# Mixer products with tokens stationary and 512 weight columns moving, and the second-last expert's combining moved into the last expert's up product

## Chip, cores and metric

One core of a Trainium2 chip runs the whole kernel in one launch. The metric is device microseconds of one execution, the median over runs. The kernel before took 1434.71 us (three runs, 1433.88 to 1435.99).

## Reference

256 tokens of width 1024 pass through one layer. A combined projection of the stream feeds three mixers (gated DeltaNet, a gated recurrent block "LRU", sliding-window attention "SWA"). Each mixer's result is projected to width 1024, multiplied by a sigmoid gate, and the sum goes through one output projection; then a layer norm, 32 experts with top-4 routing, and a last sublayer. Cut to what matters here:

```python
proj = h @ w_in
(qa, ka, va, za, aa, ba, xl, gl, qc, kc, vc, gate_logits) = split_cols(proj, IN_SPLITS)
y_a = gdn_branch(qa, ka, va, za, ...) @ w_o_gdn      # ends: o * rms(o) * norm_w * silu(z)
y_b = lru_branch(xl, gl, ...) @ w_o_lru
y_c = swa_branch(qc, kc, vc, ...) @ w_o_swa
g_a, g_b, g_c = jnp.split(jax.nn.sigmoid(gate_logits), 3, axis=-1)
y = (g_a * y_a + g_b * y_b + g_c * y_c) @ w_out
x = layer_norm(DEEPNORM_ALPHA * x + y, ...)
# then per token: sum over its 4 experts of gate * (clamped_swiglu(x @ w_gu[e] + b_gu[e]) @ w_down[e] + b_down[e])
```

## The kernel before

**Numbers as two halves.** Each fp32 operand of a mixer product is split into a rounded part (HI, xh, ...) and the rest (LO, xl, ...), both of type fp32r; a product is three matmuls: hi by hi, hi by the tokens' rest, the weights' rest by hi.

**Units.** `column` (L341) makes one unit of PE work: 128 columns of a 1024-row weight matrix are the stationary operand, k block by k block, and all 256 tokens move, so 8 x 3 = 24 matmuls of 256 columns go into one PSUM tile `pjt` (two buffers, pool `pj`). The result has weight columns on partitions and tokens along the free side. There are 117 units in a fixed order (L1195 to L1230): the input columns of the mixers, gate 1, `w_o_lru`, VA, gate 2, `w_o_swa`, six of gate 0, eight z columns, two of gate 0, eight of `w_o_gdn`, and eight of the output projection. The last (`out_unit`, L1086) already holds 128 tokens stationary and moves 256 columns of `w_out`.

**What a unit needs and leaves.** SyncE loads each unit's 512 KB piece three ahead (`load`, L361) into four buffers `w`; `split` (L369) makes HI on ACT and LO on DVE (640 columns) and POOL (384), into a ring of three. After a unit its evacuation runs: `evac_gate` (a tanh on ACT into `TG`), `evac_merge` (two DVE operations that gate and add into `MG`; for the last branch also the split into MH and ML), `evac_z` (gating by silu(z), split into AH and AL), or the residual and norm statistics of `out_unit`.

**What sets the order.** `run` (L384) writes the program out unit by unit: first the evacuation of the unit before, then the split of the piece for two units later, then the 24 matmuls, then one step of each "strand" (attention, the DeltaNet chunks, norms, router), which puts small PE work between units. Where a unit is marked `drain` (first of `w_o_gdn`, first output unit), all pending evacuations are written out ahead of it. Each engine executes its own list in that order:

```python
for u in range(-2, len(units) + 1):
    steps(pend)                       # evacuation of unit u-1, first part
    ... load(done + 3); split(...)    # piece for unit u+2
    products(ps)                      # 24 matmuls
    steps(strands)                    # small work between units
```

**Turns.** `normed` (L876) ends the DeltaNet heads: it norms rows in token layout and turns them by four transposes of 128x128 to the column layout, four times.

**Experts.** After the router, `moe` streams 32 experts' weights, 12.6 MB each, through ten buffers of 2 MB: four of them (`F`) are filled during the mixer (`prefetch`), six (`w5` to `w0`) lie on mixer memory and are loaded when that is free. Per expert `expert` (L1406) does the up product (64 matmuls of 512 columns), the activation, the down product (32 matmuls); `spread` (L1473) brings the result back to its tokens by six matmuls per half of the tokens and adds it into Y. The spread of expert e-1 is done inside expert e: the first half between the up product and the first turn, the second between the two halves of the down product (`fill`, L1582).

Of the kernel before, what the change touches and what calls it, by code (L numbers as in the profile page):

```python
# [111 lines left out]
def mixer(mx, tc, nc, a, xs, rt, dram, cst, ones, el):  # L112
# [6 lines left out]
    pj = mx.enter_context(tc.tile_pool(name="pj", bufs=2, space=PSUM))  # L119
# [34 lines left out]
    banks = Slots([bank(i) for i in range(6)])  # L154
# [14 lines left out]
    lns = mpa.tile([P, 2, 4, 6], F32, name="lns")  # L169
# [171 lines left out]
    def column(src, c0, bh, bl, evac, needs=(), drain=False):  # L341

        hl, i = [], (len(units) + 2) % 3

        def dst():
            hl.extend((HI[:, i], LO[:, i]))
            return hl

        def products(ps):
            b = [f() for f in (bh, bl)]  # L350
            for k in range(KD):
                for n, (l, r) in enumerate(((0, 0), (0, 1), (1, 0))):
                    pe.matmul(ps, hl[l][:, k], b[r][:, k], start=k == 0 and n == 0, stop=k == KD - 1 and n == 2)  # L353

        order.append((len(pieces), len(units) - 2))
        pieces.append((src[:, :, c0:c0 + P], dst))
        units.append((products, evac, needs, drain))
# [3 lines left out]
    def load(n):  # L361
        if n < len(order):
            i = order[n][0]
            raw[i] = wp.tile([P, KD, P], F32, name="w", tag="w")
            sync.dma_start(raw[i], pieces[i][0])
# [3 lines left out]
    def split(i):  # L369
# [3 lines left out]
        n = share[0]  # L373
        if n:
            dve.tensor_sub(lo[:, 0:n], s[:, 0:n], hi[:, 0:n].bitcast(F32))  # L375
        if n < KD:
            pool.tensor_tensor(out=lo[:, n:], in0=s[:, n:], in1=hi[:, n:].bitcast(F32), op=ALU.subtract)  # L377
# [6 lines left out]
    def run():  # L384
        pend, done = [], 1
        for u in range(-2, len(units) + 1):
            cur[0] = u
            if u < len(units) and u >= 0 and units[u][3]:
                steps(strands)
                for g in pend:  # L390
                    for _ in g:
                        pass
                pend = []
# [6 lines left out]
            if 0 <= u < len(units):  # L400
                products, evac, needs, _ = units[u]
                assert all(n in events for n in needs), (u, needs)
                ps = pj.tile([P, T], F32, name="pjt", tag="pj")
                products(ps)
                pend = [evac(ps)]
# [80 lines left out]
    def evac_gate(b):  # L486
        def f(ps):
            if b == 0:
                M["TG"] = big("TG", [P, KD, T])
            act.activation(M["TG"][:, b], ps, AF.Tanh, scale=0.5)  # L490
# [3 lines left out]
    def evac_merge(b, first=False, last=False):  # L494
        def f(ps):
            if b == 0 and first:
                M["MG"] = big("MG", [P, KD, T])
            if b == 0 and last:
                M["MH"] = big("AT", [P, KD, T], F32R)
                M["ML"] = big("U", [P, KD, T], F32R)  # L500
            tg, dst = M["TG"][:, b], M["MG"][:, b]
            if first:
                dve.scalar_tensor_tensor(dst, tg, 1.0, ps, ALU.add, ALU.mult)
                return
            dve.scalar_tensor_tensor(tg, tg, 1.0, ps, ALU.add, ALU.mult)
            dve.tensor_add(dst, dst, tg)
            if last:
                yield
                act.copy(M["MH"][:, b], dst)
                dve.tensor_sub(M["ML"][:, b], dst, M["MH"][:, b].bitcast(F32))  # L510
            yield
# [364 lines left out]
    def normed(t, h4, o, on=None):  # L876
# [9 lines left out]
        if on is None:  # L886
            on = yield from rows_.take()
# [3 lines left out]
        yield  # L891
        ps = yield from banks.take()
        for i in range(4):
            pe.transpose(ps[:, i * P:(i + 1) * P], on[:, i], ident)
        yield
        rows_.done(on)
        act.copy(KQ[:, c0, 0, t * P:(t + 1) * P], ps.rearrange("p (h c) -> p h c", h=4))
        banks.done(ps)
# [124 lines left out]
    def evac_z(b):  # L1023
        def f(ps):
# [726 lines left out]
```

## Time and profile before

| | |
|---|---|
| median of 3 runs | 1434.71 us |
| profiled execution | 1434.07 us |
| its span, first to last instruction | 1432.3 us |
| PE busy | 1348.4 us (94%), 8472 matmuls |
| DVE, ACT, POOL busy | 607.2, 374.6, 248.7 us |
| mean granted TensorE clock | 0.987 |
| moved | 481.77 MB, mean 336 GB/s |

Stages, by the units' start: mixer products from 9.8 to 456 us, norm and router to 469 us, experts to 1389 us, the last sublayer to the end. Busy time of PE is modelled: matmuls overlap, so the distance from start to start tells what one costs, and the mean time of one is longer than that.

### The profile page before, as it was taken

Reading aid. Unit: us, or ns where it says so; the run is one execution under the profiler, and the core shown is the slowest. Engines: PE = TensorE matmul, PEld = TensorE weight load, DVE = VectorE, ACT = ScalarE, POOL = GpSimd, SP = SyncE. Lnnn points to the kernel's source line nnn. Section 1 sums busy time; section 2 is a strip of 40 time slices with the busy share of each in tenths; the row PEclk is TensorE's granted clock in tenths of the full one; section 3 lists DMA queues with packets and bytes.
Section 4 is the critical chain, followed back from the end, with each engine's and each line's share of the span. In section 5 each row is a group of like instructions: output and inputs, shape, how many; then the busy total and the mean of one; then the engine's idle time right before and its main releaser. Section 6 shows DMA issues by size and latency. Waiting matters only on the chain. (4 is left out here: it accounts for less than half of the span.)

```text
span 1432.3 us, 20918 instructions
## 1 busy us (share of the span) xinstructions
PE 1348.4 (94%) x8472; PEld 788.8 (55%) x8473; DVE 607.2 (42%) x1289; ACT 374.6 (26%) x771; POOL 248.7 (17%) x217
## 2 busy tenths in 40 slices
PE   8989989999999899999999999999999999889987
PEld 7989988899988433433433333333333433333335
DVE  6497984865585222322322222223222322222238
ACT  6766464644551110110110111011100110011121
POOL 5654864434561000000000000000000000000000
PEclk9999999999999899999999999999999999999999
DMA  8745565445898799999999999999999999999970
GB/s 257 220 134 136 128 183 159 119 132 178 262 293 327 305 416 428 427 429 427 430 426 428 428 429 428 427 430 428 428 427 427 430 429 427 428 426 430 429 330 30
DMA packets 171292, 481.77 MB, mean 336 GB/s; under 512 B 11340, under 2 KB 134876, under 8 KB 137784
## 3 DMA queue, kind: packets, MB, share of 16 engines
q1 hardware_dynamic: 169592, 477.16, 84.6%
q0 software_dynamic: 848, 1.86, 0.4%
q8 instruction: 68, 1.11, 0.3%
q10 hardware_dynamic: 752, 1.38, 0.3%
q14 instruction: 32, 0.26, 0.0%
HBM read 478.78 MB, written 3.42 MB: 337 GB/s over the span
## 5 line engine op out<-in xcount | busy, mean ns | idle before, releaser
L1419 PE MATMUL gu<-w,xe 128*64 128x512 f32 x1168 | 262.9, 598 | 6.9 <-DMA w<-in_w_gu_dram 6.9
L353 PE MATMUL pjt<-xh,HI 128*128 128x256 f32 x680 | 199.8, 294 | 12.7 <-DVE cv L419 6.1
L1419 PE MATMUL gu<-F,xe 128*64 128x512 f32 x880 | 199.1, 596 | 5.0 <-DMA F<-in_w_gu_dram 5.0
L377 POOL TENSOR_TENSOR LO<-w,HI 128x384 fp32r<-128x384 f32 (+1 forms) x111 | 166.4, 1501 | 174.9 <-ACT HI L372 172.0
L353 PE MATMUL pjt<-xh,LO 128*128 128x256 f32 x680 | 193.6, 285 | 2.6 <-DVE LO L375 2.5
L353 PE MATMUL pjt<-xl,HI 128*128 128x256 f32 x680 | 193.4, 284 | 0.0
L1419 PEld LDWEIGHTS gu<-w,xe 128*64 128x64 f32 x1168 | 81.8, 137 | 165.6 <-issue 144.4
L1437 DVE TENSOR_SCALAR gc<-gu 128x256 f32<-128x256 f32 x64 | 27.0, 422 | 273.2 <-PE gu L1419 273.2
L353 PEld LDWEIGHTS pjt<-xh,HI 128*128 128x128 f32 x680 | 131.3, 193 | 18.3 <-issue 4.7
L375 DVE TENSOR_TENSOR LO<-w,HI 128x640 fp32r<-128x640 f32 (+1 forms) x111 | 112.8, 1017 | 62.2 <-ACT HI L372 60.7
L1350 POOL DMA_DIRECT2D pt<-in_p_dram x1 | 0.8, 779 | 789.7 <-DVE lc L1441 789.7
L353 PEld LDWEIGHTS pjt<-xh,LO 128*128 128x128 f32 x680 | 131.3, 193 | 3.1 <-DVE LO L375 2.7
L353 PEld LDWEIGHTS pjt<-xl,HI 128*128 128x128 f32 x680 | 131.5, 193 | 0.3
L1454 PE MATMUL dn<-w,hT 128*64 128x512 f32 x560 | 128.5, 601 | 1.5 <-ACT hT L1447 1.5
L1490 DVE TENSOR_TENSOR Y<-Y,cb 128x512 f32<-128x512 f32 x124 | 79.5, 683 | 114.2 <-PE cb L1479 114.2
L372 ACT CAST HI<-w 128x1024 fp32r<-128x1024 f32 x111 | 115.5, 1041 | 43.2 <-PE pjt L353 17.7
L1419 PEld LDWEIGHTS gu<-F,xe 128*64 128x64 f32 x880 | 60.4, 137 | 119.6 <-issue 105.6
L1454 PE MATMUL dn<-F,hT 128*64 128x512 f32 x464 | 106.0, 598 | 0.0
L1438 ACT ACTIVATE sg<-gc 128x256 f32<-128x256 f32 x64 | 26.8, 419 | 285.0 <-DVE gc L1437 285.0
L1382 PE MATMUL gat<-oh,xs 128*128 128x128 f32 x512 | 76.3, 294 | 24.8 <-DVE oh L1390 20.0
L1382 PEld LDWEIGHTS gat<-oh,xs 128*128 128x128 f32 x512 | 64.4, 197 | 44.5 <-issue 27.8
L1427 DVE TENSOR_TENSOR gt<-gwt,gt 128x256 fp32r<-128x256 f32 x32 | 13.6, 425 | 152.2 <-ACT gt L1426 152.2
(404 smaller groups left out, 1622.0 us busy)
## 6 DMA issues: line engine op xcount, KB each, us to landing
w<-in_w_gu_dram SPq DMA_DIRECT2D x73, 2048.0 KB, 29.2
F<-in_w_gu_dram SPq DMA_DIRECT2D x51, 2048.0 KB, 29.5
w<-in_w_down_dram SPq DMA_DIRECT2D x70, 1024.0 KB, 19.1
F<-in_w_down_dram SPq DMA_DIRECT2D x58, 1024.0 KB, 20.8
w<-in_w_in_dram SPq DMA_DIRECT2D x85, 512.0 KB, 3.7
F<-in_w_gu_dram SPq DMA_DIRECT2D x8, 1024.0 KB, 6.0
w<-in_w_o_lru_dram SPq DMA_DIRECT2D x8, 512.0 KB, 4.5
w<-in_w_o_swa_dram SPq DMA_DIRECT2D x8, 512.0 KB, 3.8
```

What stands on the lines that cost most here:

```text
L353: pe.matmul(ps, hl[l][:, k], b[r][:, k], start=k == 0 and n == 0, stop=k == KD - 1 and n == 2)
L372: act.copy(hi, s)
L375: dve.tensor_sub(lo[:, 0:n], s[:, 0:n], hi[:, 0:n].bitcast(F32))
L377: pool.tensor_tensor(out=lo[:, n:], in0=s[:, n:], in1=hi[:, n:].bitcast(F32), op=ALU.subtract)
L1350: pool.dma_start(pt, a["p"][0, 0].rearrange("(t p) c -> p t c", p=P))
L1382: pe.matmul(ps[:, kk], xs[:, t, k * P:(k + 1) * P], oh[:, t], start=t == 0, stop=t == 1)
L1419: pe.matmul(gu[64 * j:64 * j + 64, b], xe[:, k], w[:, j * D + b * 512:j * D + (b + 1) * 512], start=False, stop=k == KD - 1)
L1427: dve.tensor_sub(gt[:, 1], ps, gt[:, 0].bitcast(F32))
L1437: dve.tensor_scalar(gc[:, c], guv[:, c, 0], 7.0, None, op0=ALU.min)
L1438: act.activation(sg[:, c], gc[:, c], AF.Sigmoid, scale=1.702)
L1454: pe.matmul(dn[64 * jj:64 * jj + 64], hT[:, 2 * hf + kk, j * 64:j * 64 + 64], w[:, kk, jj * 512:(jj + 1) * 512], start=hf == j == kk == 0, ...
L1490: dve.tensor_add(y, y, pss[jj])
```

## The change

Gates, the three merge products, z and the output projection (64 of 117 units) get a new shape: 128 tokens are the stationary operand and 512 weight columns move. A piece is 256 rows by 512 columns (`wide` makes four units of 12 matmuls for 512 output columns and both token halves, with one evacuation after the fourth). PSUM is divided anew: `pj` has three tiles of 512 (two of 256 before), the strands five banks (six). Results now have tokens on partitions, so the DeltaNet rows stay as they are (`normed` loses its transposes), and `evac_z` and the last `evac_merge` turn their results with four times four transposes each. The output units mix token halves, column halves and k blocks so that the first use only the k blocks of the first half of the merge; the two drains are gone. In the last expert the spread of the expert before moves from `fill` into the up product, after k = 3 and k = 5.

```diff
-    pj = mx.enter_context(tc.tile_pool(name="pj", bufs=2, space=PSUM))
+    pj = mx.enter_context(tc.tile_pool(name="pj", bufs=3, space=PSUM))
...
-    banks = Slots([bank(i) for i in range(6)])
+    banks = Slots([bank(i) for i in range(5)])
...
+    def rows_by(ps, t, kp, b, hl, first=0, last=3):
+        for kk in range(2):
+            for n, (l, r) in enumerate(((0, 0), (0, 1), (1, 0))):
+                pe.matmul(ps, b[r][:, 2 * kp + kk, t * P:(t + 1) * P], hl[l][:, kk * 512:(kk + 1) * 512],
+                          start=kp == first and kk == n == 0, stop=kp == last and kk == 1 and n == 2)
...
+            def products():
+                b = [f() for f in (bh, bl)]
+                if kp == 0:
+                    pss.extend((psum(), psum()))
+                for t in range(2):
+                    rows_by(pss[t], t, kp, b, hl)
+                return pss
+
+            piece(src[:, 2 * kp:2 * kp + 2, c0:c0 + 512], n_ - 2, dst)
+            units.append((products, evac if kp == 3 else idle, needs[kp]))
...
-            if u < len(units) and u >= 0 and units[u][3]:
-                steps(strands)
-                for g in pend:
-                    for _ in g:
-                        pass
-                pend = []
...
+    def evac_gate(c):
+        def f(pss):
...
+            for t in range(2):
+                act.activation(M["TG"][:, t, halves[c]], pss[t], AF.Tanh, scale=0.5)
...
+            for t in range(2):
+                tg, dst = M["TG"][:, t, halves[c]], M["MG"][:, t, halves[c]]
+                if first:
+                    dve.scalar_tensor_tensor(dst, tg, 1.0, pss[t], ALU.add, ALU.mult)
+                else:
+                    dve.scalar_tensor_tensor(tg, tg, 1.0, pss[t], ALU.add, ALU.mult)
+                    dve.tensor_add(dst, dst, tg)
+            yield
+            for t in range(2 if last else 0):
+                b = yield from banks.take()
+                for i in range(4):
+                    pe.transpose(b[:, i * P:(i + 1) * P], M["MG"][:, t, (4 * c + i) * P:(4 * c + i + 1) * P], ident)
+                ps, q = b.rearrange("p (k t) -> p k t", k=4), slice(t * P, (t + 1) * P)
+                hi = M["MH"][:, 4 * c:4 * c + 4, q]
+                act.copy(hi, ps)
+                dve.tensor_sub(M["ML"][:, 4 * c:4 * c + 4, q], ps, hi.bitcast(F32))
...
-        dve.tensor_tensor(out=on, in0=ov, in1=bc(oss[:, t, c0]), op=ALU.mult)
+        dve.tensor_tensor(out=KQ[:, c0, 0, t * P:(t + 1) * P], in0=ov, in1=bc(oss[:, t, c0]), op=ALU.mult)
...
-        for i in range(4):
-            pe.transpose(ps[:, i * P:(i + 1) * P], on[:, i], ident)
...
+                act.activation(th, z, AF.Tanh, scale=0.5)
+                dve.scalar_tensor_tensor(th, th, 1.0, z, ALU.add, ALU.mult)
+                dve.tensor_tensor(out=th, in0=th, in1=o, op=ALU.mult)
+            yield
+            for t in range(2):
+                b = yield from banks.take()
+                for i in range(4):
+                    pe.transpose(b[:, i * P:(i + 1) * P], rows[t][1][:, i], ident)
...
+    for c, kp, u in ((1, 0, -6), (1, 1, -4), (0, 0, -2), (0, 1, -1), (0, 2, 0), (0, 3, 1), (1, 2, 2), (1, 3, 3)):
+        piece(wout[:, 2 * kp:2 * kp + 2, halves[c]], S + u, held_piece(kp) if c else ring_piece(kp))
...
+    for work, done in ((both(0), ()), (both(1), ()), (second(0, 0, 1), ()), (both(2), ()), (both(3), ((0, 0), (1, 0))),
+                       (second(0, 2, 3), ((0, 1),)), (second(1, 0, 1), ()), (second(1, 2, 3), ((1, 1),))):
+        units.append(out_unit(work, done))
...
+            if e == NE - 1 and k in (3, 5):
+                spread(*prev, k // 5)()
...
-                if prev is not None:
+                if prev is not None and e < NE - 1:
                     pending.append(spread(*prev, 0))
...
-            elif prev is not None:
+            elif prev is not None and e < NE - 1:
                 spread(*prev, 1)()
```

How the lists of two engines change. First DVE at the end of `w_o_gdn` and the start of the output units; L375 (after: L426) is a split, L505 and L506 (L552 and L553) gate and add into MG, L510 (L562) makes ML in the tile U. Before, every unit of 24 matmuls has one such set:

```order
L375 TENSOR_TENSOR LO<-w,HI 128x640
L375 TENSOR_TENSOR xl<-w,xh 128x5x128
L510 TENSOR_TENSOR U<-MG,AT 128x256
L505 SCALAR_TENSOR_TENSOR TG<-TG,pjt 128x256
L506 TENSOR_TENSOR MG<-MG,TG 128x256
L375 TENSOR_TENSOR LO<-w,HI 128x640
L510 TENSOR_TENSOR U<-MG,AT 128x256
```

Now one set of four 512-wide operations stands after four units, and ML follows from a turned PSUM tile (`pg`):

```order
L552 SCALAR_TENSOR_TENSOR TG<-TG,pjt 128x512
L553 TENSOR_TENSOR MG<-MG,TG 128x512
L552 SCALAR_TENSOR_TENSOR TG<-TG,pjt 128x512
L553 TENSOR_TENSOR MG<-MG,TG 128x512
L426 TENSOR_TENSOR LO<-w,HI 128x640
L426 TENSOR_TENSOR xl<-w,xh 128x640
L426 TENSOR_TENSOR LO<-w,HI 128x640
L562 TENSOR_TENSOR U<-pg,AT 128x4x128
L426 TENSOR_TENSOR LO<-w,HI 128x640
L562 TENSOR_TENSOR U<-pg,AT 128x4x128
```

The pieces of `w_out` (xl here) no longer come two to a unit, and a merge no longer stands in front of every split. Second, PE in the last expert (gu: up product, gwt and tr: turns, cb<-ob,gt: spread, dn: down product), before and now:

```order
L1419 MATMUL gu<-F_9849,xe 64x512 x4
L1419 MATMUL gu<-F_9864,xe 64x512 x8
L1419 MATMUL gu<-w_9874,xe 64x512 x8
L1479 MATMUL cb<-ob,gt 128x512 x6
L1446 MATMUL tr<-cst,lc 128x128 x2
L1454 MATMUL dn<-w_9884,hT 64x512 x8
L1446 MATMUL tr<-cst,lc 128x128 x2
L1479 MATMUL cb<-ob,gt 128x512 x6
L1454 MATMUL dn<-w_9887,hT 64x512 x8
```

```order
L1485 MATMUL gu<-F_8988,xe 64x512 x4
L1545 MATMUL cb<-ob,gt 128x512 x6
L1485 MATMUL gu<-F_9013,xe 64x512 x8
L1545 MATMUL cb<-ob,gt 128x512 x6
L1485 MATMUL gu<-w_9033,xe 64x512 x8
L1512 MATMUL tr<-cst,lc 128x128 x2
L1520 MATMUL dn<-w_9043,hT 64x512 x8
L1512 MATMUL tr<-cst,lc 128x128 x2
L1520 MATMUL dn<-w_9046,hT 64x512 x8
```

Both spreads now stand between the up product's weight rows, and none between activation and down product.

## Rows read from the trace of the kernel before

**Rows 1.** Busy time by stage (columns as its second line names them), three stretches.

```profile
core 0: us, PE busy (x) PEld busy (x) DVE busy (x) ACT busy (x) POOL busy (x), PEclk, DMA share, GB/s
460.00:480.00 20.00, 18.38 (x88) 13.53 (x90) 6.44 (x36) 3.38 (x9) 0.56 (x1) 0.67 0.59 242
...
600.00:800.00 200.00, 193.71 (x980) 77.69 (x978) 56.56 (x130) 23.82 (x61) 0.00 (x0) 1.00 1.01 428
...
1200.00:1380.00 180.00, 165.40 (x790) 60.67 (x792) 43.91 (x100) 19.96 (x49) 0.78 (x1) 1.00 1.01 427
```

**Rows 2.** Timeline of the DMA queue of SyncE, last mixer loads to first reuse.

```profile
449.49 7.31 SPq L1309 DMA_DIRECT2D w<-in_w_gu_dram  x4
477.88 6.00 SPq L1321 DMA_DIRECT2D F<-in_w_down_dram  x4
```

**Rows 3.** Timeline of PE, gate 0 units: start, busy us, line, operation, count.

```profile
364.68 0.28 PE L353 MATMUL pjt<-xh,HI 128*128 128x256 f32 x1
...
367.56 0.28 PE L353 MATMUL pjt<-xh,HI 128*128 128x256 f32 x1
...
370.44 0.60 PE L894 MATMUL pg<-cst,F 128*128 128x128 f32 x4
370.79 0.36 PE L353 MATMUL pjt<-xh,HI 128*128 128x256 f32 x1
...
373.75 0.28 PE L353 MATMUL pjt<-xh,HI 128*128 128x256 f32 x1
```

**Rows 4.** Timeline of PE in the last sublayer: fp32r matmuls of 512 and 256 columns.

```profile
1399.22 7.74 PE L1654 MATMUL gu<-F,w 128*128 128x512 f32 x32 [0.24 <-ACT w L1644]
...
1412.15 4.82 PE L1654 MATMUL cb<-F,w 128*128 128x512 f32 x20
...
1417.74 2.56 PE L1654 MATMUL cb<-F,w 128*128 128x256 f32 x20
```

**Rows 5.** Timeline of PE: starts of the seventh z unit and second output unit.

```profile
391.03 0.34 PE L353 MATMUL pjt<-xh,HI 128*128 128x256 f32 x1
...
434.85 0.28 PE L1091 MATMUL pjt<-HI,AT 128*128 128x256 f32 x1
```

**Rows 6.** Waits of PE, 388 to 436 us: total, times, longest.

```profile
PE pjt L1091 <- ACT AT L509: 1.2, 1, 1.2
PE pjt L353 <- DVE TG L505: 1.1, 2, 0.7
PE pjt L353 <- DVE th L1032: 0.9, 3, 0.3
```

**Rows 7.** Timeline of DVE and ACT: operations 512 wide, and one slow 256-wide.

```profile
388.76 1.24 DVE L1036 TENSOR_TENSOR KT<-th,RV 128x256 fp32r<-128x256 f32 x1
...
1390.14 0.69 DVE L1490 TENSOR_TENSOR Y<-Y,cb 128x512 f32<-128x512 f32 x1 [0.59 <-PE cb L1479]
...
1397.99 0.59 ACT L1366 COPY w<-cb 128x512 f32<-128x512 f32 x1 [3.47 <-PE cb L1365]
```

**Rows 8.** Waits of PE, 178 to 300 us.

```profile
PE pjt L353 <- DVE LO L375: 2.5, 1, 2.5
...
PE pjt L353 <- ACT TG L490: 1.6, 2, 1.2
```

**Rows 9.** Timeline of DVE after the last output product.

```profile
456.07 0.42 DVE L1095 SCALAR_TENSOR_TENSOR xs<-xs,pjt 128x256 f32<-128x256 f32 x1 [2.78 <-PE pjt L1091]
456.53 0.43 DVE L1096 BATCH_NORM_STATS2 lns<-xs 128x6 f32<-128x256 f32 x1
```

**Rows 10.** Timeline of PE in the last expert.

```profile
1372.99 3.65 PE L1419 MATMUL gu<-w,xe 128*64 128x512 f32 x16 [0.43 <-DMA w<-in_w_gu_dram]
1376.57 0.97 PE L1479 MATMUL cb<-ob,gt 64*128 64x512 f32 x6
...
1378.58 0.48 PE L1446 MATMUL tr<-cst,lc 128*128 128x128 f32 x2 [1.04 <-DVE lc L1441]
...
1383.59 0.96 PE L1479 MATMUL cb<-ob,gt 64*128 64x512 f32 x6
...
1384.48 3.65 PE L1454 MATMUL dn<-w,hT 128*64 128x512 f32 x16
```

More of the change, by code (lines that the diff above doesn't have):

```diff
@@ L339, in mixer, with ring, piece, psum @@
     units, pieces = [], []
-    def column(src, c0, bh, bl, evac, needs=(), drain=False):
-        hl, i = [], (len(units) + 2) % 3
+    def ring(i):
+        i = (i + 2) % 3
+        return [v[:, i].rearrange("p k c -> p (k c)") for v in (HI, LO)]
+    def piece(src, at, dst):
+        order.append((len(pieces), at))
+        pieces.append((src, dst))
+    def psum():
+        return pj.tile([P, 512], F32, name="pjt", tag="pj")
+    def column(src, c0, bh, bl, evac, needs=()):
+        n_ = len(units)
+        hl = []
@@ new lines, in idle, with wide, unit, dst @@
+    def idle(ps):
+        return
+        yield
+    def wide(src, c0, bh, bl, evac, needs=((), (), (), ())):
+        pss = []
+        def unit(kp, n_):
+            hl = []
+            def dst():
+                hl.extend(ring(n_))
+                return hl
+            def products():
+                b = [f() for f in (bh, bl)]
[6 more added lines that the diff above has]
+            units.append((products, evac if kp == 3 else idle, needs[kp]))
+        for kp in range(4):
+            unit(kp, len(units))
@@ L1084, in norm_rows @@
         M["xT"] = big("MG", [P, KD, T])
[L1086 to L1107 removed]
+    out_ps = {}
@@ new lines, in out_unit, with products, evac @@
+    def out_unit(work, done):
+        def products():
+            b = (M["MH"], M["ML"])
+            for t, c, kp in work:
+                if (t, c) not in out_ps:
+                    out_ps[t, c] = psum()
+                hl = [v[:, (kp % 2) * 1024:(kp % 2 + 1) * 1024] for v in M["wo", kp // 2]] if c else M["ring", kp]
+                assert f"m{t}{kp // 2}" in events
+                rows_by(out_ps[t, c], t, kp, b, hl)
+        def evac(_):
+            for t, c in done:
+                xv = xs[:, t, halves[c]]
+                dve.scalar_tensor_tensor(xv, xv, 2.0 * ALPHA, out_ps[t, c], ALU.mult, ALU.add)
+                dve.bn_stats(lns[:, t, c], xv)
+                if c == 0 and t == 0:
+                    for i in range(2):
+                        M["rps", i] = yield from banks.take()
+                    M["wk"] = wp.tile([P, KD * P], F32, name="wk", tag="w")
+                    pool.memset(M["wk"][:, 0:80], -3.0e38)
+                if c:
+                    dve.bn_aggr(mv[:, t, 0:2], lns[:, t])
+                    dve.tensor_scalar(mv[:, t, 2:3], mv[:, t, 1:2], 4 * LN_EPS, None, op0=ALU.add)
+                    pool.tensor_tensor(out=mv[:, t, 2:3], in0=mv[:, t, 2:3], in1=mhalf[:, 0:1], op=ALU.pow)
+                    spawn(first_norm(t))
@@ L1210, in mixer @@
     gate_units(1)
-    for b in R8:
-        column(wo["w_o_lru"], b * P, *B, note("wol" if b == 7 else "", evac_merge(b, first=True)), needs=("lru",))
+    for c in range(2):
+        wide(wo["w_o_lru"], c * 512, *B, note("wol" if c else "", evac_merge(c, first=True)), needs=(("lru",),) * 4)
     for b in R8:
```

173 lines of the change are left out of this document (67 added, 106 removed).

## The prediction

> **What bounds the kernel.** I read the stages first [rows 1]. In the expert stage the DMA engines are full: share 1.01 at 428 GB/s between 600 and 800 us, the same at 427 until 1380, while PE has gaps. Nothing that the change does alters those bytes, so the experts keep their length, and what can move is the time at which their stream starts and what follows its end. The DMA queue shows the start [rows 2]: after four loads at 449.49 us nothing is issued until 477.88, when the first early buffer has been used by expert 0. In that gap the DMA engines run at a share of 0.59 [rows 1]: the buffers are full and the stream waits for PE. So the stream starts when expert 0 does, and expert 0 waits for the mixer's last product, the norm and the router. Whatever PE saves in the mixer moves everything behind it, one for one.
>
> In the mixer PE is the pace where the change works. A gate unit starts at 364.68 and the next at 367.56 us [rows 3]: 2.88 us for 24 matmuls, 0.120 us each, without a gap. The clock there is at its 2.4 GHz level, at which 256 columns take 0.1067 us, so 0.0133 us of each is not columns.
>
> **The sum, step by step.** It is made against the profiled execution, 1434.07 us, which is 0.64 below the median 1434.71.
>
> *Matmul shape.* 64 units of 24 are 1536 matmuls of 256 columns; now 768 of 512, with the same columns in all. Before: 1536 x 0.120 = 184.3 us. The nearest row for the new shape is the last sublayer, also fp32r, 128x128 stationary and 512 moving [rows 4]: 20 of them in 4.82 us, the last lasting 0.395, so (4.82 - 0.395)/19 = 0.233 each. In the same rows 20 of 256 columns take 2.56 us, (2.56 - 0.28)/19 = 0.120, which is the mixer's own number, so the row is comparable. 768 x 0.233 = 178.9 us: **-5.4 us**. Bounds: none if 512 cost twice 256 (0.240); -10.2 us if the 0.0133 us belongs to each instruction and is paid half as often (0.2267 each).
>
> The Trainium skill, "TensorE: Matmul & The Clock Gate", section "Back-to-back issue gap", gives N/2.4 + 2.5 ns, hence 109.2 ns for 256 columns and 215.8 for 512; by it the change saves 2.6 ns a pair, 2.0 us in all, and the sum would come out 3.4 us higher. The trace does not agree with its 256-column figure: 120 ns here.
>
> *Transposes.* z's sixteen take the place of the sixteen in `normed`: nothing. The last merge adds sixteen, in four groups. A group of four costs its unit 370.79 - 367.56 - 2.88 = 0.35 us and delays the next unit, 373.75 - 370.79 - 2.88 = 0.08 [rows 3]: 4 x 0.43 = **+1.7 us**.
>
> *Stalls around z, `w_o_gdn` and the first output unit.* From 391.03 to 434.85 us [rows 5] there are 13 units, 43.82 us where 13 x 2.88 = 37.44 would do: 6.4 us lost. The waits that end last are on DVE for z and the merges and on ACT for the split of the last merged block [rows 6]. All three come from evacuating after every unit, and from the drain. With 512-wide evacuation once in four units, output pieces spread over ten units, and output units that begin on the half already merged, I let all of it go. What is late next is the PSUM tile: a wide unit takes two of three tiles, so the second tile of the next must be free after its first six matmuls, 6 x 0.233 = 1.4 us. The evacuation that frees it is one 512-wide operation, 0.59 us on ACT or 0.69 on DVE, for z both [rows 7]; that is inside 1.4 us, but DVE also has slow executions (1.24 us for 256 columns, [rows 7]). For the 14 wide products I put back 0.15 us each, 2.0 us. Net **-4.4 us**; bounds -6.4 (none put back) and 0.
>
> *Gate 1 and `w_o_lru`.* Between 178 and 300 us PE waits 1.6 us for the tanh of a gate on ACT and 2.5 us for a split on DVE [rows 8]. With two evacuations instead of eight I let half of the first go: **-0.8 us**. The second is DVE's own pace; if DVE sets the stretch, these 16 units cannot give their share of the shape, 16/64 of 5.4, which is the bound on the other side, +1.3 us.
>
> *PSUM banks, pieces and queues.* Five banks for the strands instead of six cost nothing in the order: every DeltaNet and attention step stands after the same or the next unit, and its cover is the unit's matmuls; without that cover a step would wait a full unit, 2.8 us. The pieces have the same 512 KB and the same split. SyncE's loads keep their order; one of the six mixer buffers is free earlier (KQ is no longer used for `w_out`), another later, since RV and KT now serve the very last output unit. The latter delays part of the four loads of 449.49 us by about 4 us, and the 21 us until 477.88 cover that [rows 2].
>
> *End of the mixer.* The last evacuation is 512 wide: one DVE operation and one statistic, 0.42 and 0.43 us before [rows 9], about 0.69 each now [rows 7]: **+0.5 us**, on the path to the router. Bound +1.5: the first token half is also finished two units before the end instead of three.
>
> *Last expert.* Before, the first spread lay under the wait for the activation: up product over at 1376.6, first turn at 1378.58 us. The second stood in the path, 1384.48 - 1383.59 = 0.89 us [rows 10]. Now both lie in the up product, whose last weights PE had waited for 0.43 us: +2 x 0.89 - 0.43 - 0.89 = **+0.5 us**. Bounds: -0.9 if the weights come so late that both are hidden, +0.9 if they come in time.
>
> Sum: -5.4 + 1.7 - 4.4 - 0.8 + 0.5 + 0.5 = -7.9 us. 1434.07 - 7.9 = **1426.2 us**.
>
> **Rivals.**
>
> *The shape gives little.* The longer run of 512-column matmuls in the same rows [rows 4] gives (7.74 - 0.40)/31 = 0.237: then the shape saves 768 x 0.003 = 2.5 us instead of 5.4, and the time is 1429.1 us. For it: that run is the longer one. Against: its first gap holds a start, and the shorter run has none. By the skill's gap above it would be 1429.6 us.
>
> *The clock takes it back.* After the last product PE has little to do until expert 0, and the granted clock falls to its 1.2 GHz level: 0.67 on average between 460 and 480 us, so half speed during 20 x 0.33/0.5 = 13 us [rows 1]. The first half's turns and router products now also lie behind the last product. If a second spell of 13 us falls on expert 0's up product, which is PE work without a wait, it costs half of it, 6.6 us: 1432.8 us, no change. For it: the spell already ends where that product begins. Against: the work of PE behind the last product becomes more, not less.
>
> *A PSUM wait takes the place of the stalls (slower).* If at each of the 14 wide products the tile came free one slow DVE operation too late, 1.24 us [rows 7], PE would wait 17.4 us where I put back 2.0: 1426.2 + 15.4 = 1441.6 us. It decides from 0.9 us per wide product on: 14 x 0.9 = 12.6, less 2.0, eats the 7.9 and 2.9 more. For it: evacuations queue on DVE and ACT behind strand work, and PE has already waited 2.5 us for DVE [rows 8]. Against: outside 178 to 212 us the longest such wait is 0.7 us [rows 6], and DVE's share of the evacuations gets smaller.
>
> **How the numbers follow.** A measurement of this kernel can tell about 0.2% from no change, 2.9 us: below 1431.8 is faster, above 1437.6 slower, counted from the median. The forecast has 0.62 (0.60 faster, 0.02 same); the smaller shape gain 0.15 (0.12 faster, 0.03 same); the clock 0.13 (0.02, 0.10, and 0.01 slower); the PSUM wait 0.10 (0.02 same, 0.08 slower). Together 0.74 faster, 0.17 same, 0.09 slower. For the range, all good ends together give -10.2 + 1.7 - 6.4 - 0.8 + 0.5 - 0.9 = -16.1; I take 1419.5, where about two thirds of the favourable part of the sum's spread is in. Above it reaches past the clock's 1432.8 to 1434.5, and leaves the PSUM wait out.
>
> **What would show it.** Right: in the gate 0 and `w_o_gdn` stretch, starts of 512-column matmuls 0.233 us apart; no PE wait over 0.3 us between the first z unit and the last output unit; the gap in SyncE's queue before the first reuse of an early buffer still there and its end near 470 us instead of 477.88; the expert stage as long as before, at 428 GB/s; the last expert's down product without a spread between its halves, with its up product longer by about 1.3 us. Wrong: starts 0.240 apart; PE waiting for ACT TG or DVE MG at the first unit of each wide product; the half-clock spell reaching into expert 0; or a stream of experts that starts earlier and ends no earlier.

## The result, and the profile after

The changed kernel takes **1420.68 us** (median of 4 runs, 1420.20 to 1421.88); the kernel before, beside it, 1435.35 (1433.88 to 1437.46). The ratio is 0.9894, 95% interval 0.9879 to 0.9909: about 1.1% or 14.7 us faster. The forecast was 1426.2, within 1419.5 to 1434.5. A second series of the unaltered changed kernel gave 1421.51 (six runs, ratio 0.991, 0.989 to 0.993). The profiled execution has a span of 1418.8 us, 13.5 less than before, and this is the difference that the stages below add up to.

First the stages (busy time by stretch, the view of [rows 1]; the last three numbers are the granted clock of TensorE, the share of the DMA engines and GB/s):

```profile
core 0: us, PE busy (x) PEld busy (x) DVE busy (x) ACT busy (x) POOL busy (x), PEclk, DMA share, GB/s
445.00:470.00 25.00, 23.08 (x116) 14.49 (x118) 6.71 (x36) 5.04 (x11) 0.56 (x1) 0.80 0.76 309
...
600.00:800.00 200.00, 195.19 (x980) 76.81 (x978) 52.33 (x120) 22.38 (x57) 0.00 (x0) 1.00 1.01 427
...
1200.00:1370.00 170.00, 155.17 (x736) 56.94 (x732) 42.63 (x96) 18.27 (x45) 0.78 (x1) 0.99 1.01 426
```

The experts run as before at a DMA share of 1.01 and 426 to 427 GB/s. The queue of SyncE (as [rows 2]) has the same picture, earlier:

```profile
432.25 9.44 SPq L1375 DMA_DIRECT2D w<-in_w_gu_dram  x4
461.98 6.00 SPq L1387 DMA_DIRECT2D F<-in_w_down_dram  x4
```

The first reuse of an early buffer comes at 461.98 instead of 477.88, 15.9 us earlier; the gap in front of it is still there, so the stream still waits for PE. The prediction had put this near 470, too late by what the mixer gained more. The timeline of PE shows the new matmuls (as [rows 3]: start, busy us, line, operation, count), first behind a group of strand work in `w_o_swa`, then from the end of the first half of gate 0 into z, last beside the transposes of z's results:

```profile
321.08 0.40 PE L377 MATMUL pjt<-LO,F 128*128 128x512 f32 x1
...
323.19 0.40 PE L377 MATMUL pjt<-LO,F 128*128 128x512 f32 x1
...
359.81 0.39 PE L377 MATMUL pjt<-LO,xh 128*128 128x512 f32 x1
...
365.25 0.39 PE L377 MATMUL pjt<-LO,xh 128*128 128x512 f32 x1
...
388.22 0.60 PE L1086 MATMUL pg<-cst,KQ 128*128 128x128 f32 x4
...
391.43 0.60 PE L1086 MATMUL pg<-cst,KQ 128*128 128x128 f32 x4
```

From gate 0 into z, 24 matmuls lie between 359.81 and 365.25: 0.2267 us each, the favourable bound of the prediction and not its 0.233. Behind the strand group 9 lie between 321.08 and 323.19: 0.2344. A group of four transposes with twelve matmuls takes 391.43 - 388.22 = 3.21 us, 0.49 more than 12 x 0.2267.

All waits of PE between 355 and 446 us (total, times, longest), where before there were those of [rows 6] and more:

```profile
PE pg L1186 <- DVE xs L1177: 0.7, 1, 0.7
```

One wait is left, and it is the norm's, behind the last product. From gate 0 to the last product PE has no wait that this view would list.

Where the 13.5 us came from, by the start of the first product matmul of each stage (profiled executions; "products over" is the end of the last one, "expert 31" the start of the last expert by its bias matmul; the labels are those of the experiments):

| us | before | after | e3b | e4 | e5b | e6 | e8 |
|---|---|---|---|---|---|---|---|
| gate 1 | 178.73 | 176.36 | 176.76 | 176.63 | 177.99 | 176.55 | 176.06 |
| VA | 251.70 | 248.56 | 251.20 | 246.59 | 246.16 | 249.21 | 242.14 |
| gate 2 | 286.26 | 280.33 | 282.71 | 278.38 | 280.22 | 280.98 | 276.44 |
| gate 0 | 355.07 | 349.15 | 352.78 | 348.36 | 347.04 | 349.81 | 344.73 |
| products over | 456.04 | 440.33 | 456.92 | 444.12 | 438.99 | 440.99 | 435.92 |
| expert 31 (bias) | 1361.13 | 1344.92 | 1362.63 | 1348.64 | 1345.03 | 1345.52 | 1342.11 |
| its own spread | 1388.88 | 1375.42 | 1390.06 | 1379.15 | 1375.56 | 1373.33 | 1369.90 |
| span | 1432.3 | 1418.8 | 1433.5 | 1422.6 | 1419.3 | 1416.8 | 1413.3 |

After against before: 5.9 us by the start of gate 0, 9.8 more by the end of the products, 0.5 more by expert 31, and then **2.75 us lost** in the last expert, from 27.75 to 30.50.

### The profile page after: what moved, and what is told of

Same layout as the page of the kernel before. It is cut to its first block, busy times and chain, and to the rows that moved or that the text cites. A ratio compares the mean times of both kernels' runs of the same rounds, so it can differ in the third digit from the quotient of the medians.

```text
span 1418.8 us, 19330 instructions
## 1 busy us (share of the span) xinstructions
PE 1343.1 (95%) x7720; PEld 748.0 (53%) x7721; DVE 591.8 (42%) x1245; ACT 372.4 (26%) x743; POOL 247.0 (17%) x217
## 5 line engine op out<-in xcount | busy, mean ns | idle before, releaser
L426 DVE TENSOR_TENSOR LO<-w,HI 128x640 fp32r<-128x640 f32 (+1 forms) x113 | 117.1, 1038 | 83.5 <-ACT HI L423 81.8
L367 PE MATMUL pjt<-xh,HI 128*128 128x256 f32 x424 | 124.7, 294 | 0.0
L367 PE MATMUL pjt<-xh,LO 128*128 128x256 f32 x424 | 120.5, 284 | 1.3 <-DVE LO L426 1.3
L367 PE MATMUL pjt<-xl,HI 128*128 128x256 f32 x424 | 120.1, 283 | 0.0
L367 PEld LDWEIGHTS pjt<-xh,HI 128*128 128x128 f32 x424 | 81.5, 192 | 1.8 <-issue 1.1
L367 PEld LDWEIGHTS pjt<-xh,LO 128*128 128x128 f32 x424 | 81.3, 192 | 2.0 <-DVE LO L426 1.9
L367 PEld LDWEIGHTS pjt<-xl,HI 128*128 128x128 f32 x424 | 81.5, 192 | 0.3
```

The source lines that it names most:

```text
L367: pe.matmul(ps, hl[l][:, k * P:(k + 1) * P], b[r][:, k], start=k == 0 and n == 0, stop=k == KD - 1 and n == 2)
```

## The experiments

Twelve runs. The kernels of one series share the runs of the kernel before: e1 to e4; the control, e5, e6, e7; e3b, e5b, e8; e9.

**e1: the spreads back, e2: the spreads alone.** The last expert after, on PE (as [rows 10]), and the granted clock while its down product begins:

```profile
1352.84 0.97 PE L1545 MATMUL cb<-ob,gt 64*128 64x512 f32 x6
...
1357.33 0.96 PE L1545 MATMUL cb<-ob,gt 64*128 64x512 f32 x6
...
1363.82 0.47 PE L1512 MATMUL tr<-cst,lc 128*128 128x128 f32 x2 [1.94 <-DVE lc L1507]
1364.81 5.32 PE L1520 MATMUL dn<-w,hT 128*64 128x512 f32 x16 [0.52 <-ACT hT L1513]
...
1371.02 3.65 PE L1520 MATMUL dn<-w,hT 128*64 128x512 f32 x16 [0.46 <-ACT hT L1513]
1375.42 1.46 PE L1545 MATMUL cb<-ob,gt 64*128 64x512 f32 x7 [0.74 <-ACT ob L1533]
```

```profile
1364.00:1369.00 5.00, 4.48 (x14) 1.38 (x15) 1.18 (x4) 0.69 (x2) 0.00 (x0) 0.66 1.01 410
```

Three things are to be seen: both spreads lie in the up product; behind it PE waits 1.94 us for the activation, where before the first spread lay and only 1.04 were left [rows 10]; and the first half of the down product takes 5.32 us where the second takes 3.65, at a mean granted clock of 0.66.

```diff
-            if e == NE - 1 and k in (3, 5):
-                spread(*prev, k // 5)()
...
-                if prev is not None and e < NE - 1:
+                if prev is not None:
...
-            elif prev is not None and e < NE - 1:
+            elif prev is not None:
```

(e1, in the changed kernel; e2 puts the same lines, with the opposite sign, into the kernel before.)

> The changed kernel with one part undone: in the last expert the spread of the expert before goes back to where it was (first half between up product and first turn, second half between the halves of the down product). Theory: the moved spread is a loss, because it lengthened the up product by 1.45 us and left PE idle behind it, where the granted clock then fell to half speed. From the start of the last expert to its own spread the kernel before took 27.75 us (1361.13 to 1388.88), the changed one 30.50 (1344.92 to 1375.42); so 2.75 us should come back, a median near 1417.9, and no half-clock stretch during the last down product. Rival (the price of the prediction, +0.5 us): 1420.2. Rival that the loss is a later arrival of the last weights: nothing changes, 1420.7, and PE waits for the last up weights.

> The kernel before with this part of the change alone: the two spreads inside the last expert's up product. Theory: about 2.75 us slower than before, 1438, with half the clock during the first half of the last down product. By the prediction's price, 0.5 us slower, 1435.8.

e1: 1418.85 us (five runs, ratio 0.9897, 0.9882 to 0.9911); e2: 1437.26 (ratio 1.0012, 1.0001 to 1.0022). In e1 the last expert takes 28.18 us to its own spread, so 2.3 of the 2.75 come back, and its down product begins at full clock. The rest is this wait for weights:

```profile
1357.77 3.65 PE L1485 MATMUL gu<-w,xe 128*64 128x512 f32 x16 [0.85 <-DMA w<-in_w_gu_dram]
```

In e2 the up product grew as in the changed kernel (19.89 us from the bias to the down product, 18.44 before), but the clock stayed up, and the last expert lost 1.08 us; 1.8 more of its 2.8 in the span arose between `w_o_lru` and VA, which the edit does not touch. So the move itself costs 1.1 us, and the fall of the clock, seen in the changed kernel, in its control and in e4, e5, e5b and e7, some 1.7 on top. In none of the seven profiles that have a spread in the wait for the activation did it fall there. The wait alone does not decide it, though: e2 has the same 1.94 us and no fall, and what else does stays open. By its ratio alone e1 isn't told from the changed kernel, whose interval is nearly the same; the two profiles, and e6 below, tell it.

**e3 and e3b: the third PSUM tile alone.** Seen from the waits, the tile looked like the source of the lead before gate 0: before, PE waited eight times for the conv of a column's unit (`cv`), 6.1 us in all, and after once, 1.4 us. Waits of PE up to 480 us, before and after:

```profile
PE pjt L353 <- DVE cv L419: 6.1, 8, 1.6
...
PE pjt L377 <- DVE cv L462: 1.4, 1, 1.4
```

```diff
-    pj = mx.enter_context(tc.tile_pool(name="pj", bufs=2, space=PSUM))
+    pj = mx.enter_context(tc.tile_pool(name="pj", bufs=3, space=PSUM))
...
-    banks = Slots([bank(i) for i in range(6)])
+    banks = Slots([bank(i) for i in range(5)])
```

> The kernel before with the PSUM division of the change alone: three product tiles instead of two, five strand banks instead of six, tiles still 256 wide and every product 24 matmuls of 256. Theory: the third tile alone is worth several microseconds, since PE no longer waits for the evacuation of the unit before last: -1.3 net up to gate 1, -2.8 in the VA columns, and up to 0.9 (z), 1.1 (merges) and 1.6 (gate 1): a median of 1428 to 1431. Rival (the prediction, which gave the division nothing in itself): 1435.

> The kernel before with three product tiles and five strand banks, a second profile. Its runs lay between 1429.6 and 1438.0 with a median like the kernel before, while the one profiled execution was the shortest of them (span 1427.8). There gate 0 began 7.2 us earlier than before, and the last product was over only 3.8 us earlier. Theory: the lead up to gate 0 is there in every run, and what differs is how much of it the merges and output units lose to evacuations and splits on DVE and ACT, which still come after every unit: gate 0 again near 348, the products' end between 452 and 457. Rival: the lead itself comes and goes: gate 0 beginning after 351.

e3: 1435.63 us median of 11 runs, 1429.58 to 1438.02, ratio 1.0005 (0.9996 to 1.0014): no gain in time, and my theory fell. Its first profile was its shortest run. The second run (1435.29) is near the median: gate 0 begins at 352.78, a lead of 2.3 us where the first had 7.2, so the lead itself comes and goes, as the rival had it; and the merges and output units then lose all of it and more, with waits which the changed kernel doesn't have (waits of PE in e3b, 355 to 457 us):

```profile
PE pjt L1091 <- DVE U L510: 2.0, 2, 1.2
PE pjt L353 <- DVE LO L375: 1.6, 2, 1.0
PE pjt L1091 <- ACT AT L509: 1.6, 1, 1.6
PE pjt L353 <- DVE KT L1036: 1.1, 1, 1.1
```

With a free tile at hand, PE waits for the split and for ML instead: 104.1 us from gate 0 to the end of the products, against 101.0 before.

**e5b: the tile away from the columns.** The counterpart, in the changed kernel: columns take only two of the three tiles.

```diff
-            b, ps = [f() for f in (bh, bl)], psum()[:, :T]
+            b, ps = [f() for f in (bh, bl)], psum(False)[:, :T]
```

(`psum` gets two tags, `pj` with two tiles and `pk` with one; False means `pj`. The wide products take all three in turn, the output half (0, 1) takes `pk`.)

> The changed kernel, but the column products use only two of the three PSUM tiles, as before the change; the wide products keep three. Theory: the columns then wait again for the evacuation of the unit before last (eight waits for conv outputs, up to 1.6 us each, in the profile of before), and of the 5.9 us by which gate 2 starts earlier in the changed kernel 3 to 5 are lost and carried to the end: 1424 to 1426. Rival (the chains on DVE set this stretch, as the third tile alone gave nothing in the timed runs): 1421.

1420.86 us (ratio 0.9899, 0.9881 to 0.9917): by the time the rival held. The profile shows two things that cancel. The columns did lose what the theory said: 1.63 us by gate 1 and 2.29 from VA to gate 2, against the changed kernel's profile. But from gate 1 to VA e5b took 68.17 us instead of 72.20: the stops described under e8 took 1.55 us there instead of 2.92, and the clock never fell, where the changed kernel had 10.2 us at half clock. So in sum the tile at the columns is worth nothing, in either direction; that the columns do not need it is not shown.

**e5: the tile away from the wide products.**

```diff
-                    pss.extend((psum(), psum()))
+                    pss.extend((psum(False), psum(False)))
```

> The changed kernel, but the wide products have only two of the three 512-wide PSUM tiles (the columns keep three, the output units theirs). It prices the rival of the prediction, a PSUM wait at each wide boundary. Theory: with both tiles taken, the next product cannot begin before the first evacuation after the last matmul, some 1.0 to 1.3 us at about 14 boundaries: 14 to 18 us slower, 1435 to 1439, with PE waiting for TG on ACT, th or TG on DVE at each. So the third tile is what made the stalls go. Rival (512-wide evacuation once in four units is enough by itself): 1421.

1433.15 us (ten runs, ratio 0.9979, 0.9967 to 0.9991), 11.6 more than the control beside it: less than the 14 expected, but most of the gain is gone. Its waits of PE, 176 to 470 us:

```profile
PE pjt L382 <- DVE cv L467: 6.3, 2, 3.6
PE pjt L382 <- ACT TG L541: 3.2, 1, 3.2
...
PE pjt L382 <- POOL LO L433: 2.7, 1, 2.7
PE pjt L382 <- DVE TG L557: 1.2, 3, 0.6
```

I had put the price at every boundary alike. It is 0.6 us at most where a wide product follows a merge, and up to 3.6 where it comes behind columns (`cv`) or a gate (`TG` on ACT); the wait for POOL is for a split, and the control has it too, 2.5 us. By stages 8.4 us against the control's profile arise before gate 0 and 2.4 from there to the last product. So this is where the third tile earns its bank, and it is the rival of the prediction that the division of PSUM averted.

**e4: 256 columns to a matmul, all else kept.**

```diff
-                pe.matmul(ps, b[r][:, 2 * kp + kk, t * P:(t + 1) * P], hl[l][:, kk * 512:(kk + 1) * 512],
-                          start=kp == first and kk == n == 0, stop=kp == last and kk == 1 and n == 2)
+                for h in range(2):
+                    pe.matmul(ps[:, h * 256:(h + 1) * 256], b[r][:, 2 * kp + kk, t * P:(t + 1) * P],
+                              hl[l][:, kk * 512 + h * 256:kk * 512 + (h + 1) * 256],
+                              start=kp == first and kk == n == h == 0, stop=kp == last and kk == 1 and n == 2 and h == 1)
```

> The changed kernel, each 512-column matmul written as two of 256 columns on the same stationary block and the same PSUM tile; all else is kept, evacuations, pieces, order, tiles. It prices the shape alone. If each pair costs 0.0133 us more everywhere (0.240 against 0.2267): +10.2, 1430.9. If that holds only where no strand work stands between the units (both gate 0 halves, z, w_o_gdn and the output units, 384 of 768 matmuls) and the rest costs the same in either shape: about +5 to +6, 1426. If the shape gives nothing: 1420.7.

1424.32 us (ratio 0.9928, 0.9914 to 0.9941), 3.6 above the changed kernel. Its PE timeline, in gate 0 and behind a strand group in `w_o_swa`:

```profile
351.95 0.40 PE L378 MATMUL pjt<-HI,xh 128*128 128x256 f32 x2
...
356.51 0.40 PE L378 MATMUL pjt<-HI,xl 128*128 128x256 f32 x2
```

```profile
320.03 0.40 PE L378 MATMUL pjt<-LO,F 128*128 128x256 f32 x2
...
322.16 0.39 PE L378 MATMUL pjt<-LO,F 128*128 128x256 f32 x2
```

A pair costs 0.240 us in gate 0 (19 pairs from 351.95 to 356.51), where one of 512 costs 0.2267; behind the strand group 0.2367 (9 pairs from 320.03 to 322.16), where one of 512 costs 0.2344. So the shape saves 0.013 us a pair in undisturbed units and 0.002 there. By stages: from gate 0 to the end of the products e4 takes 95.76 us and the changed kernel 91.18, 4.58 more for 384 pairs; in gate 2 and `w_o_swa` 69.98 against 68.82, 1.16 more for 192 (0.83 of it in gate 2). In gate 1 and `w_o_lru` e4 was 2.2 us the faster; the changed kernel's profile has 10.2 us at half clock in there and e4's none, and this is why the time differs by less than the 5.7 of the other stages.

**e6: one spread in the up product, one in the wait for the activation.**

```diff
-            if e == NE - 1 and k in (3, 5):
-                spread(*prev, k // 5)()
+            if e == NE - 1 and k == 5:
+                spread(*prev, 0)()
...
-                if prev is not None and e < NE - 1:
-                    pending.append(spread(*prev, 0))
+                if prev is not None:
+                    pending.append(spread(*prev, int(e == NE - 1)))
```

> The changed kernel unaltered, as the standard for the three beside it on the same chip. Expected 1420 to 1422 by every theory.

> The changed kernel with the last expert's spreads placed otherwise: the first half behind k = 5 of the up product, where PE waited 0.85 us for the last weights when both spreads were back at their old places; the second half between up product and first turn, where PE waits for the activation anyway. Theory: the first costs 0.89 less 0.85, the second nothing, and PE is not idle for 1.94 us behind the up product. From the start of the last expert to its own spread 27.9 us in place of 30.50 in the changed kernel's profile (28.18 with the spreads back): 0.3 us under that variant, and 1 to 2.6 us under the changed kernel, by whether its clock falls there: 1418.1 to 1419.7. Rival (placing does not matter, the last weights set the end): as the changed kernel.

1418.43 us (ratio 0.9884, 0.9865 to 0.9903) beside the control's 1421.51: four of its five runs lie between 1417.49 and 1418.51, and none of the control's six is under 1420.82. The last expert of e6:

```profile
1356.87 0.96 PE L1545 MATMUL cb<-ob,gt 64*128 64x512 f32 x6
1357.80 3.65 PE L1485 MATMUL gu<-w,xe 128*64 128x512 f32 x16
1361.38 0.96 PE L1545 MATMUL cb<-ob,gt 64*128 64x512 f32 x6
1363.39 0.47 PE L1512 MATMUL tr<-cst,lc 128*128 128x128 f32 x2 [1.05 <-DVE lc L1507]
1364.38 3.65 PE L1520 MATMUL dn<-w,hT 128*64 128x512 f32 x16 [0.52 <-ACT hT L1513]
```

The first spread fills the wait for the weights, the second the one for the activation, the clock stays up, and the last expert takes 27.81 us to its own spread.

**e7: the decay chain two units later.** In the changed kernel's profile the lead of the first columns ends at two waits for the DeltaNet decay chain, 1.70 us for DVE and 1.96 for ACT, between 104 and 113 us. Two more units of products are put in front of them:

```diff
         yield
+        yield
         p2 = yield from banks.take()
         pe.matmul(p2[:, 0:16], cen, flat(g), start=True, stop=True)
...
         yield from wait("G")
+        yield
         dts = []
```

> The changed kernel with the DeltaNet decay chain stretched by two units: its small matmuls (cumulative sums, decay rows) come one unit later each, so the work that they wait for on DVE and ACT has a unit's products to hide under. In the changed kernel PE waits there 1.70 us (DVE) and 1.96 us (ACT) between 104 and 115 us and the clock then runs at half for 3.4 us. Theory: the third tile let PE run ahead of this chain, and gives the gain back there; with the chain later 3 us or more stay, 1417.7 or less, gate 1 starting near 173 instead of 176.4. Rival (DVE itself is the pace between 80 and 115 us): PE waits for DVE one unit later, and for the splits behind it; 1420.7.

1421.35 us (ratio 0.9898, 0.988 to 0.9915): no change. Both waits went, and `w_o_lru` began at 202.95 us instead of the control's 207.15. Of these 4.2 us 3.2 are left at VA, 1.5 at `w_o_swa` and still at the end of the products, and 0.4 in the span; the half-clock spell behind the mixer lasted 13.7 us here and 10.2 in the control. The stop that e8 treats is not where the lead went: it took 3.18 us here, and 3.11 in the control.

**e8: the burst cut in two (with the spreads of e6).** The inverse of the DeltaNet chunks issues 256 matmuls of 32x32 in a row. In the changed kernel:

```profile
222.51 0.36 PE L777 MATMUL pg<-RV,KT 32*32 32x32 f32 x21
225.79 1.64 PE L777 MATMUL pg<-RV,KT 32*32 32x32 f32 x105 [2.92 <-issue]
```

```profile
224.00:232.00 8.00, 6.21 (x126) 4.06 (x127) 1.95 (x5) 2.27 (x4) 1.48 (x4) 0.57 0.33 94
```

PE stops after some 150 of them for 2.92 us; "issue" means that it waited for no engine or transfer that the view can name. The stretch around it has a granted clock of 0.57.

```diff
                 pe.matmul(view(b1, 16)[q, s], U0[q, s], Xn[q, s], start=True, stop=True)
+        yield
         for s in range(16):
```

> The changed kernel with the last expert's spreads placed as in e6, and with the burst of 256 matmuls of 32 x 32 in the DeltaNet inverse cut in two: 128 of them one unit later. In the changed kernel PE stops for 2.92 us inside this burst, with nothing in the profile that it waits for, and the granted clock is at half for 6.8 us around it. Theory: PE takes these tiny matmuls faster than its own instructions arrive, and with a unit's products between the halves the stop goes: 2.9 us, and up to 3.4 of the half clock: 1412 to 1416. Rival: the stop belongs to this place in the instruction stream and moves to the second half: 1418.4 as e6.

```profile
222.37 1.29 PE L774 MATMUL pg<-KT,RV 32*32 32x32 f32 x128
229.09 1.20 PE L778 MATMUL pg<-RV,KT 32*32 32x32 f32 x119
230.94 0.28 PE L778 MATMUL pg<-RV,KT 32*32 32x32 f32 x9 [0.64 <-issue]
```

1415.2 us (ratio 0.9859, 0.9841 to 0.9876), 3.2 under e6; the two intervals overlap, but the slowest of its four runs (1415.53) is under the fastest of e6's five. Of the stop 0.64 us is left, the half clock around it is gone, and VA begins 7.1 us earlier than in e6, the end of the products 5.1, expert 31 3.4.

What PE waits for in such a stop can be read from the traces. The page of the profile lists a DMA queue named "instruction" (packets, MB, share; before, then after), and the kernel before stops too, twice (its waits of PE, 178 to 300 us):

```profile
q8 instruction: 68, 1.11, 0.3%
...
q8 instruction: 62, 1.02, 0.3%
```

```profile
PE pg L1007 <- issue: 2.5, 1, 2.5
...
PE pg L723 <- issue: 0.7, 1, 0.7
```

Each packet has 16384 bytes, and there is one for every 256 records of PE (matmuls, weight loads and the like: 17178 in the profile before, 15647 after). All 20 stops of this kind over 0.25 us in the fourteen profiles stand at the same counts of PE's records, 256 apart, whatever line stands there, and each ends 1.2 to 1.5 us after the end of the 13th, 14th or 15th packet:

| profile | records of PE ahead | stop, us | packet over | PE goes on |
|---|---|---|---|---|
| before | 3777 | 0.68 | 226.23 | 227.57 |
| before | 4033 | 2.45 | 229.80 | 231.30 |
| after | 3522 | 2.92 | 224.56 | 225.79 |
| e5b | 3521 | 0.77 | 223.53 | 224.85 |
| e6 | 3522 | 3.12 | 225.13 | 226.51 |
| e8 | 3778 | 0.64 | 229.71 | 230.94 |
| e9 | 3778 | 1.18 | 227.46 | 228.87 |

Where PE passes such a count without a stop, its packet has been over for 1.4 us (once each in e8 and e9) or for 1.8 and more. So the theory of e8 holds: PE used its instructions up before the next ones had arrived. The 0.64 us left in e8 stand at the next of these counts, so the rival, that the stop belongs to a place in the instruction stream, was half right. The kernel before loses as much to it in all (3.1 us) as the changed one (2.9), so the change neither brought the stop nor took it away. What starts a packet, and why the same burst stops for 0.7 us in one kernel and for 3 in another, stays open.

**e9: e6, e7 and e8 together.**

> The changed kernel with the spreads as in e6, the inverse's burst cut in two as in e8, and the decay chain two units later as in e7. e7 by itself had w_o_lru begin 4.2 us earlier than the unaltered kernel beside it, and lost most of it at the burst (a stop of 3.18 us) and before w_o_swa. Theory: the burst was where that lead went; with the burst cut, about 3 us of it stay: 1411.5 to 1413. Rival (the chains on DVE and ACT absorb any lead before gate 0, as they did with the third tile): 1415, as e8.

1412.92 us (ratio 0.9839, 0.9822 to 0.9855; runs 1411.24 to 1415.47). Against e8's 0.9859 the intervals overlap, and in the profiles both have expert 31 begin at 1342.1 us (the profiled execution is the longest of e9's five), so whether e7's part adds anything is not settled. Either beats both kernels of this case: 5.5 to 7.8 us under the changed one.

## Why the prediction was right, and where its terms were off

The direction, the range and the mechanism held: PE's gain in the mixer moves the stream of experts one for one (products over 15.7 us earlier, first reuse 15.9, expert 31 16.2), and the bytes keep their time (903.46 us from expert 0's bias to expert 31's before, 903.68 after). Of the size the prediction had little more than half: 8.5 us under the median shown against 14.0. That the time lies within the range, 1.2 us above its lower end, is in part luck: the gain before gate 0 was not foreseen, and the last expert took part of it back. The sum beside the stages of the two profiles:

| term | forecast | measured | from |
|---|---|---|---|
| matmul shape | -5.4 | -5.7 | e4: 4.58 + 1.16, without gate 1 and `w_o_lru` |
| transposes | +1.7 | +1.7 | eight groups for four at 0.43, their price before and in e4 (0.49 beside 512 columns, which is in the row above) |
| stalls, gate 0 to the last product | -4.4 | -6.4 | units longer than 2.88 us by a wait: 6.38 before, none after |
| work that left this stretch | 0 | -1.8 | 0.97 of a DeltaNet group, now ahead of gate 0; 0.79 of the norm's turns, now behind the last product |
| before gate 0, without the above | -0.8 | -3.5 | -5.92 + 1.16 + 1.29 (three of the four old groups of transposes stood here) |
| end of the mixer to expert 31 | +0.5 | -0.5 | 16.2 less 15.7 |
| last expert | +0.5 | +2.75 | 30.50 less 27.75 |
| sum | -7.9 | -13.4 | -13.5 by the spans |

*Shape: near in sum, wrong in kind.* The forecast is for 768 pairs, the measured 5.7 for 576 of them. The 0.233 lies between two cases. Undisturbed units have 0.2267, which was the bound, and those behind strand work in `w_o_swa` 0.2344 against 0.2367, nearly no gain. The rival that the shape gives little is out where nothing disturbs, true of `w_o_swa` (0.33 us for 96 pairs), and half true of gate 2 (0.83). In undisturbed units 256 columns more cost 0.2267 - 0.1200 = 0.1067 us, so 0.0133 us of either shape belongs to the instruction.

*Stalls around z, `w_o_gdn` and the first output unit: mis-sized.* The reading of 6.4 us lost was right, and all of it went. The failing step was "For the 14 wide products I put back 0.15 us each, 2.0 us" (2.1 by its own numbers). The profile has no wait to put back. The rival's wait exists, but only without the third tile: e5 lost 11.6 us, of the order of the 15.4 of that rival. Its counterargument, "outside 178 to 212 us the longest such wait is 0.7 us", was read from 388 to 436 us alone: PE had waited 1.6 us for the conv of a column, at the end of the VA columns, and right there e5 lost most. How the 6.4 us divide between the later evacuation, the dropped drains and the new order of the output units was not tried.

*Gate 1 and `w_o_lru`: the term that failed.* "I let half of the first go: -0.8" looked only at two waits of 178 to 300 us. The view that it read [rows 8] also lists PE's two stops of 2.5 and 0.7 us, and these were left out. The stops for instructions and the half clock about them vary between kernels, and with them the time from gate 1 to VA: 72.97 us before, 72.20 after, 69.96 in e4, 68.17 in e5b, 66.08 in e8. Before and after, the stops took nearly the same (3.1 and 2.9 us), and the half clock more after (10.2 us against 6.8). The changed kernel's own lead of 5.9 us contains 1.1 of a faster first unit, and 4.1 that look like the third tile's in the columns; e5b lost 3.9 of these and got as much back behind them, so what the tile is worth here in time is not shown. How much of the -3.5 is the wide gate 1 and `w_o_lru`, and how much the chance of clock and stop, stays open.

*Last expert: the other failing term, to the other side.* "Now both lie in the up product": the lengthening was right (1.45 us, forecast 1.3). Wrong was to count the second spread's 0.89 as saved whole: without it PE waits 0.46 for the transposed activation. And the cover that I named for the first spread, the wait for the activation, was also what kept PE busy: without it the clock fell in the down product, in six profiles of seven.

*The clock's rival* did not come where I looked. The half-clock spell behind the mixer lasted 10.2 us (446.6 to 456.8) against 13.7 before, and ended before expert 0's first product at 457.0:

```profile
446.00:457.00 11.00, 9.45 (x46) 8.84 (x46) 5.29 (x34) 1.94 (x6) 0.56 (x1) 0.53 0.97 415
```

In e1, e5, e5b, e7, e8 and e9 it lasted 13.7 us and reached 0.6 to 2.2 us into expert 0. It may take part of a gain: e8's products end 5.1 us before e6's, but its spell lasts 13.7 us, e6's 10.2, and expert 31 starts 3.4 earlier.

## What to carry to other kernels

Where PE is the pace and waits for the evacuation after every small product, the larger product with one evacuation and a spare PSUM tile can be worth more than the shorter instruction stream of the wide matmul: here 6.4 us against 4.6 in the same stage, and 11.6 lost in the whole kernel without the spare tile for the wide products. Before a piece of work is moved out of a wait, ask what that wait was covering: put one piece into each wait (weights, activation), not both into one. A lead gained early is worth nothing until it has been followed to the end, past every chain and burst behind it: two local gains (e3, e7) gave no time. And where PE stops with no engine to blame, count its instructions and look at the queue that brings them; cutting one burst of tiny matmuls in two (e8) gave 3.2 us.

## What the runs showed of the hardware that I had not expected

- PE can run out of instructions. In a burst of 256 matmuls of 32x32, some 10 ns apart, it stops for 2.9 to 3.3 us in the changed kernel, its control, e1, e3b, e5, e6 and e7, for 1.3 in e2, and for 0.7 to 0.8 in the kernel before, e3, e4 and e5b; these last and e2 stop again 256 records later, for 0.8 to 2.5 us. Every such stop ends 1.2 to 1.5 us after a packet of 16384 bytes on the instruction queue. The Trainium skill, "Runtime: NRT & Kernel Launch", section "Instruction fetch mechanics", says that an engine's fetch of instructions is mostly hidden because dispatch is slower than the fill. These traces do not agree for this burst: its stops took 3.1 us before and 2.9 after.
- The spacing of fp32r matmuls depends on where they stand: 512 columns take 0.2267 us in undisturbed units and 0.2344 behind 128-column fp32 work in `w_o_swa`; 256 columns 0.1200 and 0.1183, the other way round. Why is not shown.
- The same code spreads differently: the kernel before with a third tile ran between 1429.6 and 1438.0 us (eleven runs; the kernel before beside it 1432.5 to 1438.0), the changed kernel within 1.7 us in its first series (in the second one run of six stood out, 1427.95).
